# Modulation units left out of three places of the streamed schedule, their transposes one step later

## The chip, the core and the metric

The kernel runs on one core of a Trainium2 chip. The metric is the device time of one execution in microseconds (us), given as the median over several runs. Five engines work side by side, each through its own list of instructions in a fixed order: PE (matmuls; PEld is its weight load), DVE (vectors), ACT (scalars), POOL and SP (which issues the DMAs here). A wait between engines is a semaphore.

## The reference

Two networks run one after the other on 256 tokens of width 1024. The first has two layers on x and a context ctx; both layers are modulated by vectors from `c` (for x) and `c_ctx` (for ctx). The change touches the first layer and the modulation of both:

```python
mod   = silu(c) @ w_ada[i] + b_ada[i]        # w_ada[i]: 1024 x 6144
mod_c = silu(c_ctx) @ w_ada[i] + b_ada[i]
sh1, sc1, g1, sh2, sc2, g2 = split(mod, 6)   # and six for ctx
h  = modulate(rms_norm(x, norm_mix[i]), sh1, sc1)      # hc likewise
# layer 0: short convolution
b_gate, c_gate, u = split(h @ conv_w_in, 3)
z = c_gate * u
y = (b_gate * conv3(z)) @ conv_w_out
x = x + g1 * y
x = x + g2 * swiglu(modulate(rms_norm(x, norm_ffn[i]), sh2, sc2), ffn_w_in[i], ffn_w_out[i])
# the same for ctx with its own vectors; layer 1 has attention in place of the convolution
```

The second network (two layers of ffn, mixer and ffn) is untouched.

## The kernel before

All matrices are float32, and each product is made of three matmuls: every operand is split into a rounded high part and a low part, and `hi*hi + lo*hi + hi*lo` is summed (L243 to L245 and L306 to L308; `whi`, `wlo` are the parts of the weights, `xh`, `xl` those of the activations). Activations lie with features on the partitions. x and ctx stand side by side as 512 columns.

**The weight stream.** `WeightStream` brings all weights in units of 128 x 1024 numbers (512 KB) in one order that `stream_specs` writes down. SP loads a unit (L90) into one of 5 raw buffers, as soon as the one used five units ago is free. `take()` (L113) splits up to two units ahead of the one it hands out, into 4 pairs of buffers: ACT casts `whi` (L106), DVE subtracts `wlo` (L107), in pieces of `ws.width` columns, 512 or 1024.

**The modulation.** The vectors come from 12 pieces of 1024 (six per layer). The first two pieces are made at once; the ten later ones pass through the same stream as 8 units each, without a split, in `ada_slow` (L462): DVE multiplies a unit by one number per partition and adds it to `ada_acc`, once for the x vector and once for the ctx vector (L473 the first of a piece, L475 the others; one vector alone for the last four pieces of layer 1). After 8 units, PE transposes the accumulators in 4 x 128 columns into a bank `pa` (L482: four sets for two vectors, in three auxiliary banks), DVE sums each bank over its columns (L484) and adds the bias (L486). `ada_slow` is a generator: `ada_at(step)` first advances the pieces that have had their 8 units, then takes the number of units that the table `ADA_UNITS` gives for this step. `ada_flush` runs what is pending to its end. The table has 80 units in all; steps are `("conv", g, n)` (third n of column group g of `conv_w_in`), `("hid", g, n)` (gate or up weights of ffn group g) and `("out", j)` (column group j of the ffn's second matrix, first part).

**The convolution.** In `conv_block`, the first four units of `conv_w_in` are used in two halves: contraction blocks 0 to 3 of the four banks `pcu`, then, after the second half of the modulated activations is made (`modulate(1)`: L433, L434 and L509 on DVE give `modA`, ACT scales in L801 and casts `xh`, DVE subtracts `xl`), blocks 4 to 7. Then come the last third of group 0 (`pb`) and the groups 1 to 3, with `z` (L855), the three taps (L858, L859) and the gate (L861) on DVE. `conv_out` multiplies by `conv_w_out`: groups 0 and 1 for both streams, groups 2 and 3 for x and then for ctx, each followed by the norm of that stream.

**A norm.** `row_stats` sums squares on PE (L361), `rstd_cols` takes the inverse root by Newton steps on DVE (L364, then L265 to L269, 128 x 2 numbers each), `rows_from_cols` writes it on a diagonal (L374) and PE spreads it over all partitions (L376). `modulate` then makes `xh` and `xl` from it (L532, ACT L534, casts). While the norm of ctx runs, PE has the matmuls of x: the first ffn group uses its weights for x first and for ctx after that.

The instructions of an engine are put in order when the program is built; moving a unit in the table therefore moves its neighbours on DVE, PE and SP too.

Of the kernel before, what the change touches and what calls it, by code (L numbers as in the profile page):

```python
# [165 lines left out]
class Net:  # L166
# [296 lines left out]
    def ada_slow(self, layer, j, vecs):  # L463


        nc = self.nc
        accs = [self.adap.tile([P, D], F32, name="ada_acc", tag=f"acc{v}") for v in range(vecs)]
        for kb in range(KB):
            w = self.ws.take()[0][:, 0, :]
            for v in range(vecs):  # L470
                c = self.sil[:, 8 * v + kb : 8 * v + kb + 1]
                if kb == 0:
                    nc.vector.tensor_scalar(accs[v], w, c, None, ALU.mult)  # L473
                else:
                    nc.vector.scalar_tensor_tensor(accs[v], w, c, accs[v], ALU.mult, ALU.add)  # L475
            yield
        col = self.small(16, "ada_sum")
        for v in range(vecs):
            for h in range(2):
                pt = self.aux_bank()  # L480
                for b in range(4):
                    nc.tensor.transpose(pt[:, b * P : (b + 1) * P], accs[v][:, (4 * h + b) * P : (4 * h + b + 1) * P], self.ident)  # L482
                o = 8 * v + 4 * h
                nc.vector.tensor_reduce(col[:, o : o + 4], pt.rearrange("p (b k) -> p b k", b=4), AX.X, ALU.add)  # L484
        bias = self.p(f"b_ada{layer}")[:, 8 * j : 8 * j + 8, None].to_broadcast([P, 8, vecs])
        nc.vector.tensor_tensor(self.mod[:, layer, 8 * j : 8 * j + 8, 0:vecs], col[:, : 8 * vecs].rearrange("p (v b) -> p b v", b=8), bias, ALU.add)  # L486
# [184 lines left out]
ADA_DIRECT = (0, 2)  # L671


ADA_UNITS = {("conv", 0, 1): 2, ("conv", 0, 2): 4}
ADA_UNITS.update({("conv", g, n): 2 for g in range(1, 4) for n in range(3)})
ADA_UNITS.update({("hid", g, n): 2 for g in range(10) for n in range(2)})
ADA_UNITS.update({("out", j): 4 for j in range(4)})


class AdaPlan:  # L680
# [6 lines left out]
    def at(self, step):  # L687
        return [next(self.units) for _ in range(ADA_UNITS.get(step, 0))]

# [72 lines left out]
def conv_block(net):  # L762
# [60 lines left out]
        net.wstat_unit(first[i], pcu[i], xh, xl, k8, 0)  # L823
    modulate(1)
    early.close()
    net.ws.width = WeightStream.UNIT
    for i in range(2):
        net.wstat_unit(net.ws.take(), pcu[i], xh, xl, k8, 4)
    with tc.tile_pool(name="hid0", bufs=1) as hp, tc.tile_pool(name="ada", bufs=2) as net.adap:
        sh = hp.tile([P, 12, 512], F32R, name="sh")  # L830
        sl = hp.tile([P, 12, 512], F32R, name="sl")
        with tc.tile_pool(name="conv", bufs=1) as zp:
            zs = [zp.tile([P, 2, T + 2], F32, name=f"z{i}") for i in range(2)]
            for z in zs:
                nc.vector.memset(z, 0.0)
            cw = net.p("conv_w")
            for g in range(4):
                if g == 0:
                    pc, pu = pcu
                else:  # L840
                    pc = [net.main_bank() for _ in range(2)]
                    net.wstat(pc, xh, xl, k8)
                    net.ada_at("conv", g, 0)
                    pu = [net.main_bank() for _ in range(2)]
                    net.wstat(pu, xh, xl, k8)
                net.ada_at("conv", g, 1)
                pb = [net.main_bank() for _ in range(2)]
                net.wstat(pb, xh, xl, k8)
                for c in range(2):
                    kb = 2 * g + c  # L850
                    z = zs[c]
                    cs = net.tmp()
                    nc.scalar.copy(cs, pc[c])
                    v = lambda t: t.rearrange("p (a t) -> p a t", a=2)
                    nc.vector.tensor_tensor(z[:, :, 1 : T + 1], v(pu[c]), v(cs), ALU.mult)  # L855
                    t = net.tmp()
                    nc.scalar.activation(v(t), z[:, :, 0:T], AF.Copy, scale=cw[:, kb : kb + 1])
                    nc.vector.scalar_tensor_tensor(v(t), z[:, :, 1 : T + 1], cw[:, 8 + kb : 9 + kb], v(t), ALU.mult, ALU.add)  # L858
                    nc.vector.scalar_tensor_tensor(v(t), z[:, :, 2 : T + 2], cw[:, 16 + kb : 17 + kb], v(t), ALU.mult, ALU.add)  # L859
                    y = net.tmp()  # L860
                    nc.vector.tensor_tensor(y, pb[c], t, ALU.mult)  # L861
                    net.split(sh[:, kb, :], sl[:, kb, :], y)
                net.ada_at("conv", g, 2)

            accs = [[], []]

            def conv_out(g, streams):
                cs = slice(streams[0] * T, (streams[-1] + 1) * T)
                ps = [net.main_bank()[:, : T * len(streams)] for _ in range(2)]
                net.wstat(ps, sh[:, :, cs], sl[:, :, cs], k8)  # L870
                for c in range(2):
                    for i, v in enumerate(streams):
                        net.gated_add(0, 2, 2 * g + c, v, both[v], ps[c][:, vsl[i]])
                        accs[v] = net.block_squares(both[v], 2 * g + c, accs[v], (None, zp)[v])

            net.ada_flush()
            net.ws.width = 512
            for g in range(2):
                conv_out(g, (0, 1))
            for half in range(2):  # L880
                net.mod_scale(0, 1, half)
            for v in range(2):
                for g in range(2, 4):
                    conv_out(g, (v,))
                net.modulate(0, 1, v, both[v], net.row_stats(accs[v]), k8, xh[:, :, vsl[v]], xl[:, :, vsl[v]])
        state = {}

        def evac(part, j, c, ps, v):
            kb = 2 * j + c
            for i in range(2) if v is None else (v,):  # L890
                net.gated_add(0, 5, kb, i, both[i], ps[:, vsl[i]] if v is None else ps)
                if part == len(FFN0_PARTS) - 1:
                    state[i] = net.block_squares(both[i], kb, state.get(i, []))
                    if kb == KB - 1:
                        if i == 0:
                            net.ada_flush()
                            for half in range(2):
                                net.mod_scale(1, 0, half)
                        net.modulate(1, 0, i, both[i], net.row_stats(state[i]), k8, xh[:, :, vsl[i]], xl[:, :, vsl[i]])

        net.ffn(xh, xl, sh, sl, FFN0_PARTS, evac, net.ada_at)
# [897 lines left out]
def network(tc, a, out, es):  # L1799
# [13 lines left out]
    net.C = cpool.tile([P, KB, T], F32, name="C")  # L1813
    net.ada_start()
    conv_block(net)

    def open_x():
# [127 lines left out]
```

## Time and profile before

| what | value |
|---|---|
| runs of the kernel before | 2063.38, 2065.8, 2066.5 us, median 2065.8 |
| profiled execution | 2063.77 us, its span 2061.9 us |
| mean granted clock of PE | 0.993 of full |
| DMA | 348.82 MB, mean 169 GB/s |

The span is the time from the first to the last instruction in the profile; the rest of an execution's time lies around it. A row of a timeline gives start, duration, engine, line, operation, output and inputs, how many instructions it holds, and in brackets how long the engine had stood idle and what ended that. Line numbers are those of the kernel before.

### The profile page before, as it was taken

To read this page: it belongs to the slowest core of one execution; us is meant where nothing else is said; L and a number is where in the kernel's file an instruction comes from. 1 tells how busy PE (TensorE), PEld (TensorE's weight loads), DVE (VectorE), ACT (ScalarE), POOL (GpSimd) and SP (SyncE) were. 2 spreads that over 40 slices of the span, in tenths; PEclk is the share of its full clock that TensorE was granted. 3 is DMA by queue.
4 is the path that set the end of the run, shared out by engine and by line. 5 is a ranking of instruction groups with operands and counts; after the bars stand their busy time and mean duration, and the time that the engine had idled before them with its cause. 6 is when DMAs were issued, how large, how long until landed. Compare 5 with 4: busy or idle time off the path is not lost. (4 is left out here: it accounts for less than half of the span.)

```text
span 2061.9 us, 31882 instructions
## 1 busy us (share of the span) xinstructions
PE 2011.6 (98%) x12318; PEld 1770.6 (86%) x12318; DVE 1497.0 (73%) x2628; ACT 1026.3 (50%) x1680; POOL 4.1 (0%) x24
## 2 busy tenths in 40 slices
PE   6999899999999999999999999999999999999999
PEld 3778887888899999888888889998888888989888
DVE  5996887665477778866587767787767776888774
ACT  4422442223255557555455546555545554675552
POOL 0000000000000000000000000000000000000000
PEclk9999999999999999999999999999999999999999
DMA  7763555576345333466565565556656556425554
GB/s 247 242 215 113 156 183 172 184 227 185 108 144 160 107 97 119 149 189 191 176 194 184 184 184 137 153 173 186 192 175 194 184 184 191 137 83 164 185 183 133
DMA packets 315080, 348.82 MB, mean 169 GB/s; under 512 B 12528, under 2 KB 299376, under 8 KB 314928
## 3 DMA queue, kind: packets, MB, share of 16 engines
q1 hardware_dynamic: 314928, 346.78, 54.5%
q8 instruction: 97, 1.59, 0.3%
q14 instruction: 55, 0.45, 0.1%
HBM read 345.68 MB, written 1.05 MB: 168 GB/s over the span
## 5 line engine op out<-in xcount | busy, mean ns | idle before, releaser
L106 ACT CAST whi<-wraw 128x512 fp32r<-128x512 f32 (+2 forms) x773 | 607.5, 808 | 735.4 <-issue 218.9
L107 DVE TENSOR_TENSOR wlo<-wraw,whi 128x512 fp32r<-128x512 f32 (+2 forms) x773 | 701.1, 921 | 365.5 <-ACT whi L106 362.3
L306 PE MATMUL pg<-x,whi 128*128 128x512 f32 x1408 | 386.9, 396 | 0.5 <-DVE x L255 0.4
L306 PEld LDWEIGHTS pg<-x,whi 128*128 128x128 f32 x1408 | 239.6, 188 | 34.1 <-DVE x L255 2.2
L306 PE MATMUL po<-s,whi 128*128 128x512 f32 x880 | 243.1, 394 | 0.0
L308 PEld LDWEIGHTS pg<-x,wlo 128*128 128x128 f32 x1408 | 213.8, 188 | 32.4
L243 PE MATMUL pm<-xh,whi 128*128 128x512 f32 (+1 forms) x576 | 218.8, 384 | 5.2 <-ACT xh L251 5.2
L308 PE MATMUL pg<-x,wlo 128*128 128x256 f32 x1408 | 221.0, 279 | 0.0
L244 PE MATMUL pm<-xl,whi 128*128 128x512 f32 (+1 forms) x576 | 219.5, 382 | 0.0
L245 PE MATMUL pm<-xh,wlo 128*128 128x512 f32 (+1 forms) x576 | 219.2, 381 | 0.0
L475 DVE SCALAR_TENSOR_TENSOR ada_acc<-wraw,sil,ada_acc 128x1024 f32<-128x1024 f32 x112 | 141.1, 1279 | 53.7 <-DMA wraw<-in_w_ada 53.6
L306 PEld LDWEIGHTS po<-s,whi 128*128 128x128 f32 x880 | 148.7, 189 | 18.1
L308 PEld LDWEIGHTS po<-s,wlo 128*128 128x128 f32 x880 | 137.5, 188 | 20.5
L308 PE MATMUL po<-s,wlo 128*128 128x256 f32 x880 | 142.5, 280 | 0.0
L243 PEld LDWEIGHTS pm<-xh,whi 128*128 128x128 f32 x576 | 109.8, 192 | 27.0 <-ACT xh L251 6.6
L244 PEld LDWEIGHTS pm<-xl,whi 128*128 128x128 f32 x576 | 110.1, 191 | 20.5
L245 PEld LDWEIGHTS pm<-xh,wlo 128*128 128x128 f32 x576 | 109.8, 191 | 20.6
L243 PE MATMUL pm<-sh,whi 128*128 128x256 f32 (+1 forms) x352 | 113.9, 323 | 0.0
L245 PE MATMUL pm<-sh,wlo 128*128 128x256 f32 (+1 forms) x352 | 113.7, 323 | 0.0
L244 PE MATMUL pm<-sl,whi 128*128 128x256 f32 (+1 forms) x352 | 113.2, 322 | 0.0
L245 PE MATMUL pm<-whi,xl 128*128 128x256 f32 x352 | 99.6, 283 | 0.0
L306 PE MATMUL pg<-xh,whi 128*128 128x512 f32 x352 | 96.6, 395 | 1.9 <-DVE xh L252 1.9
(431 smaller groups left out, 3387.2 us busy)
## 6 DMA issues: line engine op xcount, KB each, us to landing
wraw<-in_ffn_w_in SPq DMA_DIRECT2D x264, 512.0 KB, 3.6
wraw<-in_ffn_w_out SPq DMA_DIRECT2D x128, 512.0 KB, 3.5
wraw<-in_w_ada SPq DMA_DIRECT2D x96, 512.0 KB, 4.5
wraw<-in_a_w_in SPq DMA_DIRECT2D x28, 512.0 KB, 3.8
wraw<-in_conv_w_in SPq DMA_DIRECT2D x24, 512.0 KB, 4.8
wraw<-in_attn_w_qkv SPq DMA_DIRECT2D x24, 512.0 KB, 4.4
wraw<-in_ffn_w_out SPq DMA_DIRECT2D x28, 256.0 KB, 2.8
wraw<-in_b_w_in SPq DMA_DIRECT2D x14, 512.0 KB, 4.2
```

The source lines that it names most:

```text
L106: self.nc.scalar.copy(hi[:, cs], raw[:, cs])
L107: self.nc.vector.tensor_tensor(lo[:, cs], raw[:, cs], hi[:, cs].bitcast(F32), ALU.subtract)
L243: mm(ps, ah, bh, start=first, stop=False)
L244: mm(ps, ah, bl, start=False, stop=False)
L245: mm(ps, al, bh, start=False, stop=last)
L306: self.nc.tensor.matmul(pss[c], hi[:, kk, cs], x2[:, done + kk], start=done + kk == 0, stop=False)
L308: self.nc.tensor.matmul(pss[c][:, 0, :], lo[:, kk, cs], x2[:, done + kk, 0, :], start=False, stop=done + kk == nblocks - 1)
L475: nc.vector.scalar_tensor_tensor(accs[v], w, c, accs[v], ALU.mult, ALU.add)
```

## The change

Four edits, all in the schedule; what is computed stays the same.

1. `ada_slow` yields once more after its eight units, so that transposes and sums are issued one step of the table later.
2. `ADA_UNITS`: none at `("conv", 0, 1)` (was 2); 3 at the last third of groups 1 and 2 (was 2); none in ffn groups 0 and 1 (were 2 + 2 each), 2 + 2 in group 10 (was none); 5 at each `("out", j)` (was 4). The sum stays 80.
3. `ws.width` is set to 1024 after the last third of group 0, not ahead of the second half of the first weights: four units are split in two pieces of 512.
4. `ada_flush` stands behind each of the first two `conv_out`, not ahead of them.

```diff
--- before.py
+++ after.py
@@ -474,6 +474,7 @@
                 else:
                     nc.vector.scalar_tensor_tensor(accs[v], w, c, accs[v], ALU.mult, ALU.add)
             yield
+        yield
         col = self.small(16, "ada_sum")
         for v in range(vecs):
             for h in range(2):
@@ -671,10 +672,10 @@
 ADA_DIRECT = (0, 2)
 
 
-ADA_UNITS = {("conv", 0, 1): 2, ("conv", 0, 2): 4}
-ADA_UNITS.update({("conv", g, n): 2 for g in range(1, 4) for n in range(3)})
-ADA_UNITS.update({("hid", g, n): 2 for g in range(10) for n in range(2)})
-ADA_UNITS.update({("out", j): 4 for j in range(4)})
+ADA_UNITS = {("conv", 0, 2): 4}
+ADA_UNITS.update({("conv", g, n): 3 if n == 2 and g < 3 else 2 for g in range(1, 4) for n in range(3)})
+ADA_UNITS.update({("hid", g, n): 2 for g in range(2, 11) for n in range(2)})
+ADA_UNITS.update({("out", j): 5 for j in range(4)})
 
 
 class AdaPlan:
@@ -823,7 +824,6 @@
         net.wstat_unit(first[i], pcu[i], xh, xl, k8, 0)
     modulate(1)
     early.close()
-    net.ws.width = WeightStream.UNIT
     for i in range(2):
         net.wstat_unit(net.ws.take(), pcu[i], xh, xl, k8, 4)
     with tc.tile_pool(name="hid0", bufs=1) as hp, tc.tile_pool(name="ada", bufs=2) as net.adap:
@@ -861,6 +861,7 @@
                     nc.vector.tensor_tensor(y, pb[c], t, ALU.mult)
                     net.split(sh[:, kb, :], sl[:, kb, :], y)
                 net.ada_at("conv", g, 2)
+                net.ws.width = WeightStream.UNIT
 
             accs = [[], []]
 
@@ -873,10 +874,10 @@
                         net.gated_add(0, 2, 2 * g + c, v, both[v], ps[c][:, vsl[i]])
                         accs[v] = net.block_squares(both[v], 2 * g + c, accs[v], (None, zp)[v])
 
-            net.ada_flush()
             net.ws.width = 512
             for g in range(2):
                 conv_out(g, (0, 1))
+                net.ada_flush()
             for half in range(2):
                 net.mod_scale(0, 1, half)
             for v in range(2):
```

Lines from L477 on are one further down in the changed kernel. On DVE, at the norm of ctx, the end of the Newton steps (`rc_t`, `rc_g`, `rcol`), before:

```order
L475 SCALAR_TENSOR_TENSOR ada_acc<-wraw,sil,ada_acc 128x1024
L268 TENSOR_TENSOR rc_t<-rc_t,rc_m 128x2
L475 SCALAR_TENSOR_TENSOR ada_acc<-wraw,sil,ada_acc 128x1024
L269 SCALAR_TENSOR_TENSOR rcol<-rc_t,rc_g 128x2
L475 SCALAR_TENSOR_TENSOR ada_acc<-wraw,sil,ada_acc 128x1024
L374 TENSOR_SCALAR t<-kc,rcol 128x128 x2
L475 SCALAR_TENSOR_TENSOR ada_acc<-wraw,sil,ada_acc 128x1024
L532 TENSOR_TENSOR t<-C,pa 128x256 x2
```

and in the changed kernel, from the same chain:

```order
L267 SCALAR_TENSOR_TENSOR rc_t<-rc_g 128x2
L107 TENSOR_TENSOR wlo<-wraw,whi 128x512
L268 TENSOR_TENSOR rc_t<-rc_t,rc_m 128x2
L269 SCALAR_TENSOR_TENSOR rc_g<-rc_t,rc_g 128x2
L267 SCALAR_TENSOR_TENSOR rc_t<-rc_g 128x2
L268 TENSOR_TENSOR rc_t<-rc_t,rc_m 128x2
L269 SCALAR_TENSOR_TENSOR rc_g<-rc_t,rc_g 128x2
L267 SCALAR_TENSOR_TENSOR rc_t<-rc_g 128x2
L268 TENSOR_TENSOR rc_t<-rc_t,rc_m 128x2
L269 SCALAR_TENSOR_TENSOR rcol<-rc_t,rc_g 128x2
L374 TENSOR_SCALAR t<-kc,rcol 128x128 x2
L533 TENSOR_TENSOR t<-C,pa 128x256 x2
```

The accumulations (L475) between the steps are gone; three splits are left in the chain, of which the rows show the last. On PE, 37 matmuls of x stand between L361 and L376 of this norm (before: 59), and 31 more of x between L376 and the first matmul of ctx (before: none).

On DVE, where the second half of the first convolution weights begins (`mod`, `modA` are the scale of `modulate(1)`), before:

```order
L107 TENSOR_TENSOR wlo<-wraw,whi 128x512 x2
L433 TENSOR_TENSOR mod<-ada_col 128x8
L473 TENSOR_SCALAR ada_acc<-wraw,sil 128x1024
L434 TENSOR_TENSOR mod<-mod,pk 128x8
L473 TENSOR_SCALAR ada_acc<-wraw,sil 128x1024
L509 SCALAR_TENSOR_TENSOR modA<-mod,pk 128x8
L475 SCALAR_TENSOR_TENSOR ada_acc<-wraw,sil,ada_acc 128x1024 x2
L252 TENSOR_TENSOR xl<-t,xh 128x512 x2
```

and in the changed kernel:

```order
L107 TENSOR_TENSOR wlo<-wraw,whi 128x512 x2
L433 TENSOR_TENSOR mod<-ada_col 128x8
L434 TENSOR_TENSOR mod<-mod,pk 128x8
L510 SCALAR_TENSOR_TENSOR modA<-mod,pk 128x8
L107 TENSOR_TENSOR wlo<-wraw,whi 128x512 x2
L252 TENSOR_TENSOR xl<-t,xh 128x512
L473 TENSOR_SCALAR ada_acc<-wraw,sil 128x1024 x2
L252 TENSOR_TENSOR xl<-t,xh 128x512
```

The scale no longer has accumulations between its steps, and the split of the next weights stands ahead of the first `xl`. On PE of the changed kernel, with buffer numbers, seven matmuls of the last third of group 0 (bank `pm_589`, weights `whi_512`, `wlo_513`) have come ahead of the second half (banks `pm_436` to `pm_439`); their end and the half's begin:

```order
L244 MATMUL pm_589<-xl_97,whi_512 128x512
L245 MATMUL pm_589<-xh_96,wlo_513 128x512
L243 MATMUL pm_589<-xh_96,whi_512 128x512
L243 MATMUL pm_436<-xh_96,whi_394 128x512
L243 MATMUL pm_437<-xh_96,whi_394 128x512
L243 MATMUL pm_438<-xh_96,whi_406 128x512
L244 MATMUL pm_436<-xl_97,whi_394 128x512
```

Before, these banks' second half came directly behind their first. On DVE, at the sums of the first piece (`ada_sum`), before:

```order
L475 SCALAR_TENSOR_TENSOR ada_acc<-wraw,sil,ada_acc 128x1024 x4
L107 TENSOR_TENSOR wlo<-wraw,whi 128x1024
L475 SCALAR_TENSOR_TENSOR ada_acc<-wraw,sil,ada_acc 128x1024
L855 TENSOR_TENSOR z_573<-pm,t 128x2x256
L475 SCALAR_TENSOR_TENSOR ada_acc<-wraw,sil,ada_acc 128x1024
L858 SCALAR_TENSOR_TENSOR t<-z_573,pk,t 128x512
L484 TENSOR_REDUCE ada_sum<-pa 128x4 x4
L859 SCALAR_TENSOR_TENSOR t<-z_573,pk,t 128x512
```

and in the changed kernel:

```order
L475 SCALAR_TENSOR_TENSOR ada_acc<-wraw,sil,ada_acc 128x1024
L252 TENSOR_TENSOR sl<-t,sh 128x512
L107 TENSOR_TENSOR wlo<-wraw,whi 128x1024
L475 SCALAR_TENSOR_TENSOR ada_acc<-wraw,sil,ada_acc 128x1024 x3
L485 TENSOR_REDUCE ada_sum<-pa 128x4 x4
L107 TENSOR_TENSOR wlo<-wraw,whi 128x1024
L487 TENSOR_TENSOR mod<-ada_sum,pk 128x16
```

The sums of the first piece moved from behind `z` and its second tap to behind three accumulations of the next piece. The sums of the second piece, in the changed kernel:

```order
L107 TENSOR_TENSOR wlo<-wraw,whi 128x1024 x2
L855 TENSOR_TENSOR z_585<-pm,t 128x2x256
L858 SCALAR_TENSOR_TENSOR t<-z_585,pk,t 128x512
L859 SCALAR_TENSOR_TENSOR t<-z_585,pk,t 128x512
L485 TENSOR_REDUCE ada_sum<-pa 128x4 x4
L107 TENSOR_TENSOR wlo<-wraw,whi 128x1024
L487 TENSOR_TENSOR mod<-ada_sum,pk 128x16
L107 TENSOR_TENSOR wlo<-wraw,whi 128x512 x2
```

They stand right behind `z` and both taps of a group; before, they stood between taps and gates of the group's second half. The sums of the third piece come between the gated adds of the first `conv_out` in the changed kernel, those of the later pieces behind a few short rows of the ffn.

On SP two loads of `w_ada` no longer stand ahead of the weights of the last third of group 0, and ten units of `ffn_w_in` follow one another where four of `w_ada` stood among them.

## The prediction

> **What bounds the kernel now.** I read the page's busy table first, then the waits of PE, then the timelines around each long wait.
>
> ```profile
> span 2061.9 us, 31882 instructions
> PE 2011.6 (98%) x12318; PEld 1770.6 (86%) x12318; DVE 1497.0 (73%) x2628; ACT 1026.3 (50%) x1680; POOL 4.1 (0%) x24
> ```
>
> PE is busy 2011.6 us, so only some 50 us of the span can be won by order alone. The waits of PE in the first 420 us (engine, tile and line, releaser: us in total, times, longest) hold nearly all of it that the change touches:
>
> ```profile
> PE pa L482 <- DVE ada_sum L484: 7.7, 4, 2.5
> PE pa L376 <- DVE t L374: 6.2, 1, 6.2
> PE pm L243 <- ACT xh L251: 5.2, 3, 2.1
> ```
>
> The first row is the transposes that close a modulation piece; the second the norm of ctx after the convolution; the third the start of a modulated half. The longest wait, in the order of time on DVE:
>
> ```profile
> 241.54 0.16 DVE L364 TENSOR_SCALAR rc_m<-pa 128x2 f32<-128x2 f32 x1 [0.55 <-PE pa L361]
> ...
> 242.90 0.15 DVE L267 SCALAR_TENSOR_TENSOR rc_t<-rc_g 128x2 f32<-128x2 f32 x1
> 242.97 1.28 DVE L475 SCALAR_TENSOR_TENSOR ada_acc<-wraw,sil,ada_acc 128x1024 f32<-128x1024 f32 x1
> 244.16 0.15 DVE L268 TENSOR_TENSOR rc_t<-rc_t,rc_m 128x2 f32<-128x2 f32 x1
> ...
> 253.03 0.15 DVE L269 SCALAR_TENSOR_TENSOR rcol<-rc_t,rc_g 128x2 f32<-128x2 f32 x1
> 253.10 1.27 DVE L475 SCALAR_TENSOR_TENSOR ada_acc<-wraw,sil,ada_acc 128x1024 f32<-128x1024 f32 x1
> 254.30 0.47 DVE L374 TENSOR_SCALAR t<-kc,rcol 128x128 f32<-128x128 f32 x2
> ```
>
> The steps of the root take 0.15 us each, and between every two stands an accumulation of 1.27 us. On PE this gives:
>
> ```profile
> 248.40 0.28 PE L245 MATMUL pm<-xh,wlo 128*128 128x256 f32 x1
> 254.92 1.19 PE L376 MATMUL pa<-t,ones 128*128 128x256 f32 x2 [6.24 <-DVE t L374]
> 258.05 1.22 PE L243 MATMUL pm<-xh,whi 128*128 128x256 f32 x4 [1.93 <-ACT xh L251]
> ```
>
> PE ran out of matmuls of x at 248.68, and ctx started at 258.05. The granted clock (the last but two number of a window's row) then shows what such a hole costs beyond itself:
>
> ```profile
> 251.05:261.29 10.24, 4.44 (x17) 3.75 (x18) 9.15 (x16) 4.68 (x11) 0.00 (x0) 0.50 0.53 159
> 261.29:264.70 3.41, 3.41 (x30) 3.41 (x30) 3.28 (x5) 2.14 (x4) 0.00 (x0) 1.00 0.13 18
> 305.67:309.08 3.41, 1.17 (x8) 0.73 (x7) 3.41 (x5) 0.00 (x0) 0.00 (x0) 1.00 0.12 41
> 309.08:312.49 3.41, 3.41 (x9) 2.64 (x8) 3.41 (x6) 0.00 (x0) 0.00 (x0) 0.50 0.44 146
> ```
>
> Half the clock was granted until 261.29, and once more from 309.08 to 312.49.
>
> **Step A, the norm of ctx.** The change takes all modulation units out of the first two ffn groups, so the eleven accumulations between 242.97 and 254.69 leave the chain; three splits (L107) stay. The norm of x shows the chain without accumulations, with two splits in it:
>
> ```profile
> 225.26 0.16 DVE L364 TENSOR_SCALAR rc_m<-pa 128x2 f32<-128x2 f32 x1 [0.62 <-PE pa L361]
> ...
> 227.37 0.69 DVE L107 TENSOR_TENSOR wlo<-wraw,whi 128x512 fp32r<-128x512 f32 x1 [0.19 <-ACT whi L106]
> ...
> 228.66 0.48 DVE L374 TENSOR_SCALAR t<-kc,rcol 128x128 f32<-128x128 f32 x2
> ```
>
> That is 3.4 us from L364 to L374; with a third split 4.1, so L374 at about 245.6 and its two halves done at 246.1. PE holds matmuls of x until 248.68; the order of the changed kernel puts 37 of them behind L361 ahead of L376 and 31 more behind it. 31 at 0.114 us (3.41 us for 30 in the full-clock window) are 3.5 us, against the 3.1 us from L376 to the first matmul of ctx in the rows above: covered, just. ctx can then start when x ends, plus L376 itself and a short wait for it: 248.68 + 0.6 = 249.3 in place of 258.05, **-8.75 us**. Half clock goes as well: the 15 matmuls from 258.05 to 261.29 took 0.216 us each, and at 0.114 cost 1.5 less. **A: -10.2** (from -8.0, if L376 waits a microsecond or more and the clock still dips, to -10.3). The same eleven accumulations run in later groups, beside full PE work: hid 10 takes the units that the first groups lose, and each step of out takes a fifth.
>
> **Step B, the second half of the first convolution weights.** Two units (two vectors each) leave this place:
>
> ```profile
> 56.82 0.74 DVE L473 TENSOR_SCALAR ada_acc<-wraw,sil 128x1024 f32<-128x1024 f32 x1
> 57.56 0.74 DVE L473 TENSOR_SCALAR ada_acc<-wraw,sil 128x1024 f32<-128x1024 f32 x1
> 58.23 0.15 DVE L509 SCALAR_TENSOR_TENSOR modA<-mod,pk 128x8 f32<-128x8 f32 x1
> 58.41 1.59 ACT L801 ACTIVATE t<-xr,mod,modA 128x256 f32<-128x256 f32 x3 [2.67 <-DVE modA L509]
> 59.91 0.60 ACT L251 CAST xh<-t 128x512 fp32r<-128x512 f32 x1
> 60.56 0.74 PE L243 MATMUL pm<-xh,whi 128*128 128x512 f32 x2 [2.06 <-ACT xh L251]
> ```
>
> Without the two L473, modA comes 1.2 us sooner (each holds DVE about 0.6 beyond the step behind it). Of the hole of 2.06 us 0.9 is left, and the order puts seven matmuls of the third part of group 0 into it, 7 x 0.222 = 1.6 us of work that is due anyway. So **B: -2.0**, the whole hole. It rests on the weights of that third part being there 10 us earlier than now. Their loads move ahead by two:
>
> ```profile
> 50.29 1.70 SPq L90 DMA_DIRECT2D wraw<-in_w_ada  x2
> 52.85 1.66 SPq L90 DMA_DIRECT2D wraw<-in_conv_w_in  x2
> wraw<-in_conv_w_in SPq DMA_DIRECT2D x24, 512.0 KB, 4.8
> ```
>
> Issued at 50.29 rather than 52.85 and landing 4.8 us on, they are in at 55.1, cast and subtracted by 57 to 58. If they come 3 us later than that, the seven matmuls block the second half behind them on PE and B is +1; bounds -2.06 and +1. The four units now split as two halves of 512 hold the same data; their four more casts and subtractions I price at nothing, since PE waits for no split of theirs.
>
> **Step C, the transposes.** There are 16 for a piece of two vectors, into three banks of which each is freed by a reduce; PE issues 12, and the last 4 wait for the first reduce. The waits were:
>
> ```profile
> 151.76 1.47 PE L482 MATMUL pa<-kc,ada_acc 128*128 128x128 f32 x12
> 108.15 0.66 PE L482 MATMUL pa<-kc,ada_acc 128*128 128x128 f32 x4 [1.95 <-DVE ada_sum L484]
> 308.39 0.66 PE L482 MATMUL pa<-kc,ada_acc 128*128 128x128 f32 x4 [2.24 <-DVE ada_sum L484]
> ```
>
> and two more, 7.7 us in all: PE came while DVE still had other rows, most of them the last accumulations, ahead of the reduce. The one at 308.39 was followed by the half clock of 309.08, in which PE did 9 matmuls in 3.41 us where 0.222 each (90 in the 20 us row below) would have been 2.0: 1.4 us lost. Before: 9.1 us. With the extra step the accumulations are done, but what stands on DVE ahead of the reduce is now other work. For the first piece the rows are a split of xl, a 1024-wide wlo and three accumulations of the next piece: between nothing (DVE has run ahead) and 0.7 + 1.2 + 3 x 1.27 - 1.5 (PE's 12 transposes, first row above) = 4.2; I take 2.1, the middle, which is also near the two waits just shown. For the second, the reduces come behind the z of the part that PE has just ended:
>
> ```profile
> 151.39 0.68 DVE L855 TENSOR_TENSOR z<-pm,t 128x512 f32<-128x512 f32 x1
> 152.87 0.75 DVE L858 SCALAR_TENSOR_TENSOR t<-z,pk,t 128x512 f32<-128x512 f32 x1
> 153.54 0.68 DVE L484 TENSOR_REDUCE ada_sum<-pa 128x4 f32<-128x512 f32 x1
> ```
>
> z to L858 is 1.5 us, L858 and L859 0.67 each, the reduce 0.68: 3.5 us after PE's last matmul, and 0.2 for the hand-overs, less 1.5 for the 12 transposes: 2.2 (up to 4.6 behind two splits). The third, behind the first conv_out, waits for two gated adds: 0.3; the next three have only short rows ahead: 0.2 each. After: 2.1 + 2.2 + 0.3 + 0.6 = 5.2. [...] Two waits of 2.1 and 2.2 fall mostly in one window 6 times in 10: 2 x 0.6 x 1.4 = 1.7. After 6.9, so **C: -2.2** (bounds -6.9 and +3.4).
>
> [...]
>
> **Elsewhere** nothing is priced. In groups 1 and 2 of the convolution a third part takes three units, 2.5 us more of DVE each (two vectors at 1.27). DVE is full there, first row below, but the stream splits two units ahead of use, and a unit is 24 matmuls or 5.3 us of PE, so 10 us of cover stand against it. The out stage is in the last row:
>
> ```profile
> 100.00:120.00 20.00, 18.05 (x88) 14.86 (x87) 19.35 (x22) 5.73 (x7) 0.00 (x0) 1.00 0.66 209
> 320.00:340.00 20.00, 20.00 (x90) 16.54 (x89) 14.32 (x18) 6.18 (x11) 0.00 (x0) 1.00 0.60 187
> 420.00:440.00 20.00, 20.00 (x90) 16.57 (x89) 12.58 (x18) 3.81 (x7) 0.00 (x0) 1.00 0.74 247
> ```
>
> DVE has 7 us of 20 free there; a fifth unit on each of four steps costs 1.3 to 2.5.
>
> **Sum:** -10.2 - 2.0 - 2.2 = -14.4. Against the profiled execution's own 2063.77 us that is 2049.4; against the median of 2065.8 it is 2051.4, and the median is what I predict.
>
> **Rivals.**
> 1. The wait moves instead of going: the first two pieces wait 4 us each for DVE (it is full from 80 to 160 us) with the clock behind, or the early third part blocks PE. C +3, or B +1 and C +1: a gain of 5 to 9, 2057 to 2061. For it: DVE's load; against: the weights' splits stand ahead. 0.13.
> 2. No transpose waits at all: C -9, a gain of 21, 2045. Against it: the second piece's reduces stand behind z in the order. 0.05.
> 3. The change doesn't do what it says: the root's chain stays late, because its three splits wait for casts on ACT or for DMA as two in the norm of x did for 0.19 us. Each late unit costs up to a load's 4.8 us, and PE has only 37 matmuls (4.2 us) ahead: A -3, total -4 to +1, 2062 to 2067. 0.08.
> 4. Slower: the out stage starves. A step of out takes 3 weight units and now 5 of modulation in 16.0 us (72 matmuls of 0.222), 8 x 0.524 MB, or 262 GB/s; the row at 420 shows 247 with 7 units. From the point where a unit takes more than 2.0 us from load to release, each of the four steps falls behind, and one that runs dry costs PE a load (4.8 us) and a dip (1.4): 4 x 6.2 = 25, less 14, 2076. For it: 262 is over any 20 us there; against: DMA is busy 0.74, so some 330 are to be had, and PE is at 20.00 of 20. 0.04.
>
> **How the numbers follow.** The forecast has 0.70, with its own range 2047 to 2057. A difference within 0.2% (4.1 us) is about what a measurement of this kernel can't tell from none. The range of 8 in 10 takes the forecast, the second rival's near end and most of the first: 2046 to 2060. Faster: 0.70 + 0.13 + 0.05 = 0.88; same: most of rival 3, 0.07; slower 0.05.
>
> **What would show it.** A: L376 waits under 1 us, the first matmul of ctx stands within 1.5 us of x's last, and the clock is full there. B: no wait of L243 for xh near 58 us, and PE matmuls of the third part ahead of the second half. C: the transposes wait 4 to 7 us in all, most in the first two pieces; the half clock comes once or twice. Wrong would be a new wait of PE for a wlo in groups 0 to 2 or in the out stage, or a transpose wait above 4 us.

## The result, and the profile after

| kernel | median of its runs | ratio to before, 95% interval | profiled execution | span |
|---|---|---|---|---|
| before | 2065.52 us (2063.38 to 2066.5) | | 2063.77 us | 2061.9 us |
| changed | 2048.09 us (2047.39 to 2048.39) | 0.9916 (0.9899 to 0.9934) | 2047.39 us | 2045.6 us |

The change saves 17.4 us by the medians and 16.4 between the two profiled executions, where 14.4 was forecast. Two rows of the changed kernel's page, its span and the busy times of the engines:

```profile
span 2045.6 us, 31905 instructions
PE 2009.8 (98%) x12318; PEld 1769.8 (87%) x12318; DVE 1497.8 (73%) x2632; ACT 1026.5 (50%) x1684; POOL 4.1 (0%) x24
```

The only row that is left of PE's waits between 50 and 410 us (us in total, times, longest):

```profile
PE pa L483 <- DVE ada_sum L485: 3.6, 2, 1.9
```

The busy times are nearly those of before (PE has 1.8 us less); what went is waiting. Both traces hold 12318 matmuls, so the start of the n-th of one can be set against the n-th of the other. The difference, cut where no set of transposes lies across the cut, gives a ledger by stage. This one (own arithmetic, us against the profiled execution of before; negative is time saved) has all the runs of this study; the head gives the stage's place in the trace of before:

```
                 start   half 2   pieces 1-3  norm ctx  pieces 4-10  rest      sum
                 to 52   52-72    72-213      213-268   268-612      612-2058
changed           +1.0    -2.4     +0.5       -10.3      -4.9        -0.2     -16.3
e9_again          +1.7    -2.4     -1.8       -10.3      -4.8        +2.3     -15.3
e1_hid            +1.5     0.0     +1.9       -10.3      +0.2        -3.2      -9.9
e2_conv           +0.3    -2.4     -1.8         0.0      -0.8        +0.1      -4.6
e3_yield           0.0    +1.6     -1.3        +0.8      -6.7         0.0      -5.6
e7_noyield        +0.1    -2.4     -1.8       -10.3      +2.3        +3.2      -9.0
e5_width          -0.3    -2.2     -1.8       -10.3      -5.4        +3.6     -16.4
e6_flush          +0.3    -2.3     -1.6       -10.3      -5.2        +3.3     -15.9
e8_hid1           +0.8    -2.4     -1.9        -6.6      -6.7        +0.8     -15.9
e4_two            +1.1    -2.4     -3.4       -10.3      -6.8        +1.6     -20.3
e10_two           +1.0    -2.4     -3.4       -10.4      -6.8        +1.5     -20.4
```

The start and the rest hold code that is the same in all of them and still move by 2 and 7 us from run to run; the four columns between repeat to 0.1 or a few tenths wherever the kernels do the same there and the clock does not dip. A dip (a stretch in which the granted clock is 0.50) shows in two places: +0.5 for pieces 1 to 3 of the changed kernel (129.26 to 132.67 us in its trace), where e9_again, the same kernel, has -1.8, and +1.6 for half 2 of e3_yield (61.91 to 65.32). The reading goes by those four.

**The norm of ctx**, in the timeline of the changed kernel, on DVE and then on PE:

```profile
239.63 0.16 DVE L364 TENSOR_SCALAR rc_m<-pa 128x2 f32<-128x2 f32 x1 [0.47 <-PE pa L361]
...
241.05 0.68 DVE L107 TENSOR_TENSOR wlo<-wraw,whi 128x512 fp32r<-128x512 f32 x1
241.66 0.15 DVE L268 TENSOR_TENSOR rc_t<-rc_t,rc_m 128x2 f32<-128x2 f32 x1
...
243.22 0.48 DVE L374 TENSOR_SCALAR t<-kc,rcol 128x128 f32<-128x128 f32 x2
...
243.97 0.59 PE L376 MATMUL pa<-t,ones 128*128 128x256 f32 x2
```

The window of 20 us around it (the clock is the last number but two):

```profile
240.00:260.00 20.00, 20.00 (x165) 19.86 (x164) 13.13 (x32) 11.12 (x23) 0.00 (x0) 1.00 0.43 126
```

From L364 to L374 it is 3.6 us instead of 12.8, L376 carries no bracket (no wait), PE is busy 20.00 of 20 us and the mean clock is 1.00.

**The second half of the first weights**, on DVE, ACT and PE:

```profile
58.17 0.17 DVE L510 SCALAR_TENSOR_TENSOR modA<-mod,pk 128x8 f32<-128x8 f32 x1
...
58.37 1.59 ACT L802 ACTIVATE t<-xr,mod,modA 128x256 f32<-128x256 f32 x3 [0.43 <-DVE modA L510]
...
60.52 0.39 PE L245 MATMUL pm<-xh,wlo 128*128 128x512 f32 x1
60.75 1.07 PE L243 MATMUL pm<-xh,whi 128*128 128x512 f32 x4
```

The row at 60.75 holds four matmuls: the last of the seven of group 0's third part and, from 60.97 on, the first three of the second half. None of them waits. By its time in the trace modA is no earlier than before (58.17 against 58.23), but this execution was 1.0 us late when it came here; against its own stream of matmuls it is 1.1 us earlier.

**The transposes**, on PE:

```profile
129.00 0.91 PE L483 MATMUL pa<-kc,ada_acc 128*128 128x128 f32 x4 [1.92 <-DVE ada_sum L485]
173.76 2.04 PE L483 MATMUL pa<-kc,ada_acc 128*128 128x128 f32 x16
350.31 0.66 PE L483 MATMUL pa<-kc,ada_acc 128*128 128x128 f32 x4 [1.68 <-DVE ada_sum L485]
```

The first and the fifth piece still wait, the second runs its 16 in one go. What the two wait for, in the timeline of DVE (first piece, then fifth):

```profile
124.68 3.66 DVE L475 SCALAR_TENSOR_TENSOR ada_acc<-wraw,sil,ada_acc 128x1024 f32<-128x1024 f32 x3
128.27 2.47 DVE L485 TENSOR_REDUCE ada_sum<-pa 128x4 f32<-128x512 f32 x4
...
348.36 0.69 DVE L252 TENSOR_TENSOR sl<-t,sh 128x512 fp32r<-128x512 f32 x1 [0.69 <-ACT sh L251]
348.97 0.68 DVE L582 TENSOR_TENSOR t<-pm,t 128x512 f32<-128x512 f32 x1
349.57 1.28 DVE L485 TENSOR_REDUCE ada_sum<-pa 128x4 f32<-128x512 f32 x2
```

The clock around the first wait, in two windows:

```profile
125.85:129.26 3.41, 1.49 (x9) 0.96 (x8) 3.41 (x5) 0.00 (x0) 0.00 (x0) 1.00 0.83 246
129.26:132.67 3.41, 3.41 (x11) 2.76 (x10) 3.41 (x7) 0.00 (x0) 0.00 (x0) 0.50 0.73 212
```

For the first piece it is the three accumulations of the next one. For the fifth it is the gated products of the ffn (L582) with a split (L252) between them, and this split waits 0.69 us for a cast on ACT.

### The profile page after: what moved, and what is told of

It is laid out like the page before. It is cut to its first block, busy times and chain, and to the rows that moved or that the text cites. A ratio compares the mean times of both kernels' runs of the same rounds, so it can differ in the third digit from the quotient of the medians.

```text
span 2045.6 us, 31905 instructions
## 1 busy us (share of the span) xinstructions
PE 2009.8 (98%) x12318; PEld 1769.8 (87%) x12318; DVE 1497.8 (73%) x2632; ACT 1026.5 (50%) x1684; POOL 4.1 (0%) x24
## 5 line engine op out<-in xcount | busy, mean ns | idle before, releaser
L106 ACT CAST whi<-wraw 128x512 fp32r<-128x512 f32 (+1 forms) x777 | 608.2, 804 | 738.8 <-issue 192.4
L107 DVE TENSOR_TENSOR wlo<-wraw,whi 128x512 fp32r<-128x512 f32 (+1 forms) x777 | 702.0, 918 | 366.3 <-ACT whi L106 362.0
L475 DVE SCALAR_TENSOR_TENSOR ada_acc<-wraw,sil,ada_acc 128x1024 f32<-128x1024 f32 x112 | 140.6, 1280 | 33.5 <-DMA wraw<-in_w_ada 33.1
```

The lines of the kernel that those rows point to most:

```text
L106: self.nc.scalar.copy(hi[:, cs], raw[:, cs])
L107: self.nc.vector.tensor_tensor(lo[:, cs], raw[:, cs], hi[:, cs].bitcast(F32), ALU.subtract)
```

## The experiments

The theory is that the gain is three separate ones, by place: the norm of ctx from the ffn part of the table, the hole at 58 us from the convolution part, the transposes from the extra step. The rivals are that one edit carries the others, or that a wait only moves.

### e1_hid, e2_conv, e3_yield: one part each on the kernel before

```diff
 # e1_hid
-ADA_UNITS.update({("hid", g, n): 2 for g in range(10) for n in range(2)})
-ADA_UNITS.update({("out", j): 4 for j in range(4)})
+ADA_UNITS.update({("hid", g, n): 2 for g in range(2, 11) for n in range(2)})
+ADA_UNITS.update({("out", j): 5 for j in range(4)})
```

> The kernel before with the ffn part of the table alone (no units in ffn groups 0 and 1, 2 + 2 in group 10, 5 at each out step). Theory, the edits add up by place: step A alone, 10.2 us forecast and 10.4 us between the two traces, so about 2055 us, no wait of L376 for the diagonal, no wait for xh behind it and full clock there, the waits of L482 still about 7 us. Rival, the gain needs the extra step too (the accumulations come back in front of other waits): a gain under 7 us, with new or longer waits of PE between 250 and 560 us.

Measured: 2055.07 us, ratio 0.9951 (0.9933 to 0.9969), its runs from 2050.34 to 2062.35. The ledger has -10.3 for the norm of ctx, as the whole change does. That the total meets the 2055 of the theory is partly luck, since other columns cancel: the rest has -3.2 with no edit in it (over the whole span the mean granted clock of this execution is 0.998, against 0.993 in the kernel before), and the transposes got worse, 10.3 us of waits in three instead of 7.7 in four. The longest, on DVE and on PE:

```profile
343.08 3.67 DVE L475 SCALAR_TENSOR_TENSOR ada_acc<-wraw,sil,ada_acc 128x1024 f32<-128x1024 f32 x3 [2.80 <-DMA wraw<-in_w_ada]
...
347.41 1.11 PE L482 MATMUL pa<-kc,ada_acc 128*128 128x128 f32 x4 [5.36 <-DVE ada_sum L484]
```

PE came to wait at 342.05 (347.41 less 5.36), while the last units of the piece were still on their way from memory. So the gain at ctx needs nothing but this part, but the part alone gives some of it back at the fifth piece.

```diff
 # e2_conv
-ADA_UNITS = {("conv", 0, 1): 2, ("conv", 0, 2): 4}
-ADA_UNITS.update({("conv", g, n): 2 for g in range(1, 4) for n in range(3)})
+ADA_UNITS = {("conv", 0, 2): 4}
+ADA_UNITS.update({("conv", g, n): 3 if n == 2 and g < 3 else 2 for g in range(1, 4) for n in range(3)})
...
-    net.ws.width = WeightStream.UNIT
...
                 net.ada_at("conv", g, 2)
+                net.ws.width = WeightStream.UNIT
```

> The kernel before with the convolution part of the table and the later switch to 1024-wide splits, nothing else. Theory: step B alone, 2.0 to 2.4 us less, so about 2063 us, the wait of 2.06 us near 58 gone and the first matmuls of the last third of group 0 in its place; the waits of the first three transposes may move by 2 us either way because the units move. Rival: the hole at 58 us only moves to the weights of the last third or to the group after it, and the time stays at 2065.

Measured: 2059.33 us, ratio 0.9969 (0.9957 to 0.9981), 5.6 us and not 2.4. The hole is worth its -2.4 in the ledger and does not move anywhere. The surplus is in the transposes: shifted units let the first three wait 1.3 us instead of 3.0 (-1.8 in the ledger), and pieces 4 to 10 have -0.8.

```diff
 # e3_yield
             yield
+        yield
         col = self.small(16, "ada_sum")
...
-            net.ada_flush()
             net.ws.width = 512
             for g in range(2):
                 conv_out(g, (0, 1))
+                net.ada_flush()
```

> The kernel before with the extra step ahead of the transposes and the flush behind the first two conv_out, the table as before. Theory, the transposes wait because they follow the last accumulations directly: some 4 to 5 us less, about 2061 us, the waits of the fourth and fifth piece (2.24 and 2.48 us) gone, one wait of about 2 us left. Rival, what frees the transposes in the changed kernel is the emptied ffn groups and not the step: less than 1.5 us of gain, L482 still waits 6 us or more.

Measured: 2058.08 us, ratio 0.9961 (0.9948 to 0.9974), 6.9 us less where 4 to 5 were forecast. The transposes wait 1.7 us in all, and -6.7 of the ledger is at pieces 4 to 10: both long waits (2.24 and 2.48 us) and the half clock behind one of them (0.50 from 309.08 to 312.49 us). The rival falls. The +1.6 at the second half is the old hole of 2.05 us, which in this execution had 3.41 us of half clock behind it:

```profile
58.50:61.91 3.41, 1.36 (x7) 1.10 (x7) 2.88 (x3) 3.41 (x7) 0.00 (x0) 1.00 1.00 353
61.91:65.32 3.41, 3.41 (x10) 2.64 (x9) 3.26 (x4) 3.41 (x7) 0.00 (x0) 0.50 0.47 159
```

In the kernel before the same hole (2.06 us) cost no clock: it is 1.00 from 50 to 60 us and from 60 to 70. Why the two differ is not shown.

The three alone save 9.9 to 10.5, 5.6 to 6.2 and 6.9 to 7.4 us by their medians (against 2064.93 in these rounds and 2065.52), 22 or more together, against 17.4. The medians don't settle whether they add, since e1_hid has -3.2 in the rest, where nothing was edited. In the four columns the three together have -18.8 us, against -17.1 and -19.3 in the two traces of the changed kernel. Place by place they don't add: e2_conv and e3_yield shorten the same waits of the first three pieces (-1.8 and -1.3 alone, -1.8 in e9_again), and e3_yield and e1_hid meet at the fifth, which waits 5.36 us in e1_hid and not at all in e3_yield (pieces 4 to 10: -7.3 for the three, -4.9 and -4.8 for the changed kernel).

### e5_width, e6_flush, e7_noyield: the changed kernel with one edit undone

In e5_width the line `net.ws.width = WeightStream.UNIT` stands again behind `early.close()`; in e6_flush `net.ada_flush()` stands again ahead of the loop over `conv_out`; e7_noyield is this:

```diff
             yield
-        yield
         col = self.small(16, "ada_sum")
```

> The changed kernel with the switch to 1024-wide splits back ahead of the second half. Theory, the hole at 58 us closes because the modulation units are gone from the queues, and the width only brings the first matmuls of the last third a little sooner: PE waits at most 0.7 us near 58, the time stays within 1 us of 2048 (a dip of the clock elsewhere aside, 1.5 us each). Rival, only the half-width split brings these weights in time: a wait of 1 to 2 us stays near 58, about 2050.

> The changed kernel with the flush back ahead of conv_out. Theory, the third piece had no wait before and has none here, so the move brings nothing: no wait of L483 between 180 and 200 us, 2048. Rival, the sums of the third piece then stand behind the last z and taps and PE waits 2 us for a bank: 2050, or 2051.5 with a dip of the clock.

> The changed kernel without the extra step ahead of the transposes. Theory: the new table makes the waits of the transposes longer where units come faster (with the ffn part alone one of them took 5.36 us, behind the last accumulations), and the step takes them away: L482 waits 7 to 10 us in all, the time 5 to 7 us over the changed kernel, 2053 to 2055. Rival, with the table alone the transposes are as cheap: L482 waits under 5 us, within 2 us of 2048.

Measured: e5_width 2046.04 us (ratio 0.991, 0.9894 to 0.9926), e6_flush 2046.74 (0.9913, 0.9896 to 0.9929), e7_noyield 2052.03 (0.9937, 0.9921 to 0.9954). Without the later switch of the width the hole at 58 us stays closed (-2.2 against -2.4), without the later flush the third piece waits as little as with it: neither edit can be told from nothing. The step is needed: without it the median is 5.3 to 6.0 us over those of e5_width and e6_flush in the same rounds. The row of PE's waits for the sums in e7_noyield, between 50 and 410 us:

```profile
PE pa L482 <- DVE ada_sum L484: 7.8, 2, 6.4
```

6.4 us is the fifth piece again: the column of pieces 4 to 10 is +2.3 instead of -4.9 (over the whole span the mean granted clock of this execution is 0.992, against 0.995 in the changed kernel's). With the new table the step decides at this piece alone. Without it the first piece waits 1.36 us, about as long as with it (1.24 in e9_again), and the second and fourth don't wait; their waits of before go with the moved units alone (the second's in e2_conv, the fourth's in e1_hid).

### e8_hid1: a smaller dose at the norm of ctx

```diff
-ADA_UNITS.update({("hid", g, n): 2 for g in range(2, 11) for n in range(2)})
+ADA_UNITS.update({("hid", g, n): 2 for g in range(1, 10) for n in range(2)})
```

> The changed kernel with 2 + 2 units back in ffn group 1 and none in group 10. Theory, every accumulation among the Newton steps of ctx delays its matmuls once PE has run out of x: two multiplications (0.67 us each) and two accumulations (1.2 us) come back ahead of the diagonal, 3.8 us, less about 1 us of cover: 2.5 to 3.5 us and perhaps a dip, 2050.5 to 2053. Rival, only the units of group 0 stood in the way: no wait of L376 and the time within 1 us of 2048.

Measured: 2046.59 us, ratio 0.9912 (0.9897 to 0.9926), by its median the rival's number. The trace says otherwise, on DVE and then on PE:

```profile
242.18 1.28 DVE L475 SCALAR_TENSOR_TENSOR ada_acc<-wraw,sil,ada_acc 128x1024 f32<-128x1024 f32 x1 [0.85 <-DMA wraw<-in_w_ada]
...
244.83 0.48 DVE L374 TENSOR_SCALAR t<-kc,rcol 128x128 f32<-128x128 f32 x2
...
245.46 0.67 PE L376 MATMUL pa<-t,ones 128*128 128x256 f32 x2 [0.50 <-DVE t L374]
248.07 1.22 PE L243 MATMUL pm<-xh,whi 128*128 128x256 f32 x4 [1.58 <-ACT xh L251]
```

Waits of 2.1 us are back, and the matmuls of 128x256 behind them stand 0.21 us apart (from 249.09 us on) where those ahead stood 0.12 apart (to 244.68), which is the dip. The norm of ctx is worth -6.6 instead of -10.3: 3.7 us, about what the dose predicts (2.5 to 3.5 us and perhaps a dip), and part of it is a load (0.85 us) that the Newton steps wait for behind an accumulation. The total hides it, because with this table the fifth piece no longer waits (-6.7 instead of -4.9), and pieces 1 to 3 have -1.9 instead of +0.5. A median that stays does not show that a cost is absent.

### e4_two, e9_again, e10_two: a version that beats both

The two waits left are waits for a bank: 16 transposes need four, and there are three (12 run, and the last 4 wait when DVE has not yet summed the first bank). One more step between the vectors asks for two at a time:

```diff
                 nc.vector.tensor_reduce(col[:, o : o + 4], pt.rearrange("p (b k) -> p b k", b=4), AX.X, ALU.add)
+            if v < vecs - 1:
+                yield
```

> The changed kernel with one more step between the eight transposes of the x vector and the eight of the ctx vector, so that no step asks for more than two of the three banks. Theory, the two waits that are left (1.92 us with a dip of the clock, 1.68 us) are waits for a bank: both go, 5 us less than the changed kernel, about 2043 us. Rival, DVE is behind by then whatever the banks: the second eight wait as the last four did, and the time stays within 1.5 us of 2048.

> The changed kernel once more, beside the next one on one chip. Theory, the dip of the clock behind the first piece's wait (129 us in its first profile) and the long half clock at the start are draws of the window's phase and no part of the change: a wait of 1.2 to 1.9 us for the first piece with or without a dip, the median between 2045 and 2049. Rival, the dip belongs to the change: it stands there again, and the median is 2048 or more.

> The kernel of e4_two once more. Theory: no wait of L483, and 3 to 5 us less than the changed kernel in the same rounds (its two waits, 1.2 to 1.9 us each, and up to one dip of 1.5). Rival, the 5 us of e4_two were mostly other dips: within 1.5 us of the changed kernel.

Measured: e4_two 2042.74 us (ratio to before 0.9888, 0.9875 to 0.9901), and in rounds of their own the changed kernel again 2046.28 (0.9909, 0.9894 to 0.9923) beside e10_two 2043.1 (0.9891, 0.9875 to 0.9908). In both traces of this version PE has no wait for a sum left. It runs eight transposes at a time, but for the third piece, which the flush ends with 16 in one go (e4_two, first and second half of the first piece):

```profile
124.71 1.03 PE L483 MATMUL pa<-kc,ada_acc 128*128 128x128 f32 x8
136.49 1.04 PE L483 MATMUL pa<-kc,ada_acc 128*128 128x128 f32 x8
```

The gain over the changed kernel is 3.2 us in the common rounds (5.3 against its first median), which the ledger puts where the waits were: pieces 1 to 3 at -3.4 and pieces 4 to 10 at -6.8, in both runs. e9_again, the changed kernel once more, has 1.24 us for the first piece's wait and -1.8 instead of +0.5 in the column, 1.6 us more than the shorter wait explains: by the ledger the dip at 129 us belongs to one execution and not to the change. The window's phase that the theory names is the author's estimate; no run shows it.

## Why the prediction was right, point by point

The 2048.09 us measured lie in the forecast's own range of 2047 to 2057, near its lower end; by the medians the gain is 3.0 us more than forecast.

- **Step A** (-10.2): -10.3 in the ledger, and the same within 0.1 in every run that has the ffn part of the table and keeps group 1 empty. The mechanism is the one named, in its parts too: three splits left in the chain, the 31 matmuls behind L376 cover the scaling, the half clock is gone (the mean clock from 240 to 260 us is 1.00, and 0.78 in the kernel before). L376 does not even wait. e8_hid1 shows it by a dose. One reading was off: ten accumulations start from 242.97 to 254.69, not eleven, and nine of them stand ahead of L374; the sum doesn't use their number.
- **Step B** (-2.0): -2.4, which is 0.3 beyond the bound of -2.06. The bracket counts only from the end of the last matmul; from start to start (58.12 to 60.56) the hole put 2.44 us where the matmuls around it stand 0.23 apart. The seven matmuls and the earlier scale fill the hole; weights came in time, and the bound of +1 did not apply. That the width helps was not claimed, and e5_width shows it does not.
- **Step C** (-2.2) is the term that was mis-sized: -4.4 in the changed kernel's first profile and -6.6 in e9_again, the difference being the dip and a first wait that was 0.7 us shorter. The 1.7 us for the clock (6 times in 10 for two waits) were the author's estimate, and no run shows that term; the first profile has one dip, 0.50 from 129.26 to 132.67 us behind the first wait, and 1.00 from 347 to 357 us around the other. Waits of 5.2 us were forecast and 3.6 came, but in other places. The first piece was nearly right (2.1 forecast, 1.92 and 1.24 measured, behind the three accumulations). The step that failed is the second piece's: "3.5 us after PE's last matmul ... less 1.5 for the 12 transposes: 2.2". It took the transposes to come when `z` starts. In the trace of the changed kernel `z` (first row, on DVE) starts 2.5 us ahead of them (they stand at 173.76 in the rows of PE above), because PE still has the twelve matmuls of the group's second bank to do. The sums (second row) start 0.6 us behind the first transpose, and no transpose waits:

```profile
171.24 0.69 DVE L855 TENSOR_TENSOR z<-pm,t 128x512 f32<-128x512 f32 x1 [0.59 <-PE pm L245]
...
174.40 2.48 DVE L485 TENSOR_REDUCE ada_sum<-pa 128x4 f32<-128x512 f32 x4
```

  The other error is the fifth piece, priced at 0.2 for "short rows": the rows are short, but one of them waits for ACT, and the wait was 1.68 us. The first error shows in the order once the matmuls that stand between are counted; the second needs the order of ACT as well. The two errors have opposite signs (2.2 too much, 1.5 too little), so it is partly luck that C is off by no more. And the extra step, from which C starts, decides at the fifth piece alone (e7_noyield). The bounds of C end at -6.9, though rival 2 has -9 for the same term.
- **Elsewhere:** nothing was priced and nothing came. With five units a step the out stage has PE at 20.00 of 20 us, here and in each window of 20 us from 385 to 485; in the one from 445 to 465 the DMA moved 314 GB/s:

```profile
405.00:425.00 20.00, 20.00 (x98) 16.69 (x97) 17.83 (x24) 3.43 (x6) 0.00 (x0) 1.00 0.70 239
```

- **Rivals:** the starved out stage and the late Newton chain did not happen (the total of -4 to +1 given for the late chain is not the sum of its terms, which is -3 - 2.0 - 2.2 = -7.2 before any late unit). The wait that moves did in part (first piece, with a dip), and was outweighed. No transpose waits at all is what e4_two makes of the kernel, and 2045 was forecast for that rival: it is at 2043.
- **The difference to the forecast,** 14.4 against 16.4 by the profiles: step C 2.2, B 0.4, A 0.1, less a start that was 1.0 us later (and 0.2 in the rest). The start ranges from -0.3 to +1.7 over the eleven traces, ahead of the first edited matmul: PE's first matmul starts at 10.8 us in the changed kernel's first profile, 11.0 in the kernel before and 12.4 in e9_again, and the half clock near 36 us lasts 6.83 us in the kernel before (36.01 to 42.84) and 10.24 in the changed one (33.69 to 43.93). Why these differ is not shown.

## What to carry to other kernels

Accumulations of 1.27 us cost nothing in the out stage, where PE is busy 20.00 of 20 us; between dependent steps of 0.15 us they made a chain 12.8 us long instead of 3.6, for which PE ran out of work and waited 6.24 us, with half clock until 261.29 us: keep fillers out of serial chains, and count the work that the bottleneck has in hand while the chain runs. Work that ends on a ring of few buffers should ask for no more of them at a time than there are: 16 transposes on three banks waited in some places and ran in one go in others, eight on two never waited. And where totals move by more than the effect, compare two traces at the same instruction count: here that settled effects of 0.3 to 4 us which the medians showed as nothing, or as something else, once dips of the clock were told apart.

## What the runs showed of the hardware

The same hole did not always cost the same. A wait of 1.73 us in the second network (with one of 0.19 shortly ahead of it), in two windows of e9_again:

```profile
842.36:845.77 3.41, 1.49 (x6) 0.84 (x5) 1.90 (x4) 3.41 (x8) 0.00 (x0) 1.00 0.03 10
845.77:849.18 3.41, 3.41 (x13) 2.94 (x13) 2.72 (x4) 3.41 (x7) 0.00 (x0) 0.50 0.00 0
```

and in two windows of the kernel before:

```profile
858.63:862.04 3.41, 2.26 (x14) 1.59 (x13) 2.50 (x5) 3.41 (x9) 0.00 (x0) 1.00 0.27 96
862.04:865.45 3.41, 2.63 (x15) 2.36 (x16) 2.37 (x4) 3.41 (x7) 0.00 (x0) 1.00 0.01 2
```

In e9_again the clock is 0.50 for 3.41 us behind the wait, in the kernel before it is 1.00 in both windows. What decides between the two is not shown. By the ledger a dip of 3.41 us cost 1.6 us in two places: half 2 of e3_yield, and pieces 1 to 3 of the changed kernel against e9_again (2.3 us, less 0.7 for the longer wait). The column of the rest, where nothing was edited, runs from -3.2 to +3.6, as much as many edits; how much of that is the clock is not shown.

Some dips follow windows in which the profile has PE busy throughout. In the kernel before PE is busy 3.42 us of 1244.32 to 1247.74 and 3.41 of 1759.74 to 1763.15, and the clock is 0.50 for 3.41 us behind each; in the changed kernel it is busy 3.41 us of 1228.36 to 1231.77 and 3.41 of 1743.77 to 1747.18, with 3.41 us at 0.50 behind each. Their cause stays open.
